# Group 0's second part moved behind group 10, and side work held to the program's order on VectorE, in a hybrid decoder layer

## The chip, the core and the metric

The kernel runs on one core of one Trainium2 chip. A core has five engines that work from queues of their own: TensorE (PE in the profile; its weight loads are PEld), VectorE (DVE), ScalarE (ACT), GpSimd (POOL) and SyncE (SP), which here issues all DMA transfers. The metric is the device time of one execution in microseconds; the time of a kernel is the median of several runs.

## The reference

One decoder layer on x of 1024 tokens by 1024 channels, float32: a first feed-forward (SwiGLU, inner width 2816) with half weight, a mixer, a second feed-forward with half weight, and a final norm. Each of the three sub-layers has a norm whose scale, shift and gate come from the conditioning vector.

```python
h = modulate(rms_norm(x, ffn1_norm[l]), sh1, sc1)
x = x + 0.5 * g1 * swiglu(h, w_gate, w_up, w_down)     # (silu(h @ w_gate) * (h @ w_up)) @ w_down
h = modulate(rms_norm(x, mix_norm[l]), sh2, sc2)
b_gate, c_gate, v, u = split(h @ w_in)
y_conv = b_gate * causal_conv3(c_gate * v)
y_ssm  = glu(gelu(s5_scan(u)))                          # diagonal complex state, 32 groups x 64 states
x = x + g2 * (concat(rms_norm(y_conv), rms_norm(y_ssm)) @ w_out)
h = modulate(rms_norm(x, ffn2_norm[l]), sh3, sc3)
x = x + 0.5 * g3 * swiglu(h, ...)
return rms_norm(x, final_norm)
```

## The kernel before

Data lies with channels on the 128 partitions and tokens along the row, in two halves of 512 tokens (`h` = 0, 1). Every float32 matrix product is three matmuls of a high and a low part (`mm3`): each weight tile and each activation is split by ScalarE (a cast to the high part) and VectorE (the rest). The weights come through `Weights`: raw arrays of 1 MB (`raw`, two buffers), split tiles of two chunks (`w`, a ring of three, with a fourth, `ring1`, in some stages), in the order in which the stages take them.

The inner width is cut into eleven groups of 256. In the first feed-forward groups 0 to 3 are plain products (`gate_up`), groups 4 to 10 use a scheme of seven products in place of eight on the two halves of tokens and of channels (`seven`; its operands are called A11, A12, A22 and S1 to S4, its PSUM banks A to E; GpSimd forms the sums of the weights). What a group gives is stored to DRAM scratch (`kept`) and fetched again (`fetch`) for the second part, the product with the down weights. Groups 1 to 8 go through `down7` in two chunks of four groups (fad0, fad1; again seven products each, for two halves p of the output columns). Groups 0, 9 and 10 go through `last_parts` (fald), three weights to one PSUM bank. Each result is added to x on VectorE with the gate. Fetched tiles lie in two pools of buffers, A (20) and B (12), which also hold the activations of the running stage.

Beside the main chain runs side work, written as Python generators: `side1` prepares the tables of the state space part (`ssm_base`, `ssm_batch`), the sums S1 to S4 of the activations (`combos`, `combos_last`), and the gate of the first feed-forward; `side2` computes scales, shifts and gates of later norms, one reduction over a loaded tile `wm` at a time (24 in the first feed-forward's second part, 24 in the mixer, the latter through two buffers). A `Clock` counts the products `mm3` as ticks; after every `period` ticks it takes one step of the side work, so that its instructions are written into the program between those of the main chain. The period is 4 in groups 1 to 3, 7.75 in groups 4 to 10, 8 in chunk 1 and in the last gates of the mixer, 1000 from the mixer's GLU to the middle of the output product, and 3 from there on.

What the program's order means: a scheduler walks the traced instructions at build time with estimated durations and fixes each engine's queue. An instruction that it finds ready may pass an earlier one of the program that waits. On the chip each queue then runs strictly in that order. The wrapper `InOrder` around each engine can bind every instruction to the one before it (`strict`, used in the prologue). Elsewhere nothing is bound: side work may pass the main chain's instructions on VectorE.

The lines in question: `Clock.step` (80), `InOrder.__getattr__` (105), `stream` (287), `seven` (575), `down7` (655), `down2` (700), the stage from line 1173 to 1237, and the mixer's side work from 1413 to 1486.

Of the kernel before, what the change touches and what calls it, by code (L numbers as in the profile page):

```python
# [21 lines left out]
P = 128  # L22
# [16 lines left out]
LAST = ((0, NGRP - 2, NGRP - 1), (NGRP - 2, NGRP - 1))  # L39
# [19 lines left out]
class Clock:  # L59
# [3 lines left out]
    def __init__(self, period):  # L63
        self.now, self.period, self.n, self.since = 0, period, 0, 0
        self.due, self.side = [], deque()
# [31 lines left out]
class InOrder:  # L97


    strict = False  # L100

    def __init__(self, tc, engine):
        self.tc, self.engine, self.last = tc, engine, None

    def __getattr__(self, name):
        def call(*args, **kw):
            r = getattr(self.engine, name)(*args, **kw)  # L107
# [124 lines left out]
def hymba_layer(ctx: ExitStack, tc, x_d, wm1_d, wmod_d, gu1_d, gs1_d, ds1_d, wl1_d, win_d, wout_d, glu_d, gu2_d, gs2_d, wd2_d, ds2_d, wl2_d, cols_d, cond_d, lam_d, bc_d, out_d):  # L232
# [54 lines left out]
    def stream(gu, gs, wd, ds, wl, m):  # L287
# [4 lines left out]
        for g in range(m, NGRP):  # L292
            j = len(srcs)
            inner = g == 1
# [14 lines left out]
    stream(gu1_d, gs1_d, None, ds1_d, wl1_d, SEVEN_FROM[0])  # L309
# [525 lines left out]
    kept = {g: kept_for(g, g not in LAST[0]) for g in range(NGRP)}  # L835
# [337 lines left out]
    movs["B"] = es1.enter_context(tc.tile_pool(name="movB1", bufs=12))  # L1173
# [7 lines left out]
    a_last = [{} for _ in LAST[0]]  # L1181
# [5 lines left out]

    def fetch_last(left):

        if left in ("A11", "A12", "A22"):  # L1190
            i = ("A11", "A12", "A22").index(left)
            for h in range(2):
                for fi in range(2):
                    a_last[i][fi, h] = fetch(kept[LAST[0][i]], f"A{h + 1}{fi + 1}", "A", f"fa{LAST[0][i]}l")

    for g in range(SEVEN_FROM[0], NGRP):
        if g == NGRP - 1:
# [14 lines left out]
    sums_open.close()  # L1212
    ring1_open = ExitStack()

    def last_parts():
        for dh in range(2):
            wd = ws.take(3)
            for h in range(2):
                outs = [ps(f"fald{4 * dh + i}_{h}") for i in range(4)]
                for q, (w, a) in enumerate(zip(wd, a_last)):  # L1220
                    for fi in range(2):
                        for i, o in enumerate(outs):
                            mm3(o[:], w, 4 * fi + i, a[fi, h], q == fi == 0, q == 2 and fi == 1)
                    if h:
                        ws.free()
                for i, o in enumerate(outs):
                    d = 4 * dh + i
                    V.scalar_tensor_tensor(out=x[d][h], in0=o[:], scalar=gate[:, 0, d : d + 1], in1=x[d][h], op0=ALU.mult, op1=ALU.add)
                    after1(d, h)

    last_parts()
# [3 lines left out]
    ring1 = ring1_open.enter_context(tc.tile_pool(name="ring1b", bufs=1, side="right"))  # L1235
    ws.open(ring1, 1)
    ws.pump()
# [247 lines left out]
    clock.period = 4  # L1485
    mods_open.close()
# [40 lines left out]
    kept = {g: kept_for(g, g not in LAST[1]) for g in range(1, NGRP - 1)}  # L1527
# [70 lines left out]
def _arrays(i):  # L1598
# [5 lines left out]
    for n in (1, 2):  # L1604
# [5 lines left out]
        if n == 2:  # L1610
            a["wd2"] = b[0].transpose(1, 2, 0, 3).reshape(P, 2, 1024)
        b = b[list(LAST[n - 1])].transpose(3, 0, 2, 1, 4).reshape(-1, 2, P, 1024)
# [30 lines left out]
_ORDER = ["x", "wm1", "wmod", "gu1", "gs1", "ds1", "wl1", "win", "wout", "glu", "gu2", "gs2", "wd2", "ds2", "wl2", "cols", "cond", "lam", "bc"]  # L1643
# [17 lines left out]
```

## Time and profile before

| what | value |
| --- | --- |
| median of three runs | 1750.19 us (1748.85 to 1751.76) |
| profiled execution | 1752.1 us |
| its span | 1750.3 us |
| granted TensorE clock, mean | 0.989 |
| TensorE busy | 1677.9 us (96%) |
| VectorE busy | 1300.6 us (74%) |
| ScalarE, GpSimd busy | 566.0 us, 351.1 us |
| DMA moved | 304.54 MB, mean 174 GB/s |

How to read it. The profile is of one execution; times in its rows count from the start of the span. The span in 40 slices gives each engine's share in tenths. The waits name who waited, for whom, how long in total, how often, and the longest. A timeline row has its start, its duration, engine, line, operation, output and inputs, and in brackets the idle time before it with what ended it. All main instructions are issued by the helper on line 107, so tiles tell them apart: fa are tiles of the first feed-forward's groups, fad and fald its second part, u, v, c, b, gl, wo the mixer's products, fb the second feed-forward. The prologue runs to 87 us, groups 1 to 10 to 505, the second part to 734, the mixer to 1076.

### The profile page before, as it was taken

To read this page: it belongs to the slowest core of one execution; us is meant where nothing else is said; L and a number is where in the kernel's file an instruction comes from. 1 tells how busy PE (TensorE), PEld (TensorE's weight loads), DVE (VectorE), ACT (ScalarE), POOL (GpSimd) and SP (SyncE) were. 2 spreads that over 40 slices of the span, in tenths; PEclk is the share of its full clock that TensorE was granted. 3 is DMA by queue.
4 is the path that set the end of the run, shared out by engine and by line. 5 is a ranking of instruction groups with operands and counts; after the bars stand their busy time and mean duration, and the time that the engine had idled before them with its cause. 6 is when DMAs were issued, how large, how long until landed. Compare 5 with 4: busy or idle time off the path is not lost.

```text
span 1750.3 us, 20808 instructions
## 1 busy us (share of the span) xinstructions
PE 1677.9 (96%) x7532; PEld 1379.6 (79%) x7532; DVE 1300.6 (74%) x2286; ACT 566.0 (32%) x934; POOL 351.1 (20%) x241
## 2 busy tenths in 40 slices
PE   4999999999999999999999899989999999999996
PEld 3788887878787888887877778778888888888886
DVE  7999999999855687744656977967777666676656
ACT  4223234444322221332113424423343443322221
POOL 0000132222222221100000022023323322333211
PEclk9999999999999999999999999999999999999998
DMA  8245544444597877134654450113444334669312
GB/s 319 85 145 196 207 167 165 182 169 178 196 391 266 326 256 292 56 84 149 210 157 140 144 191 25 48 46 135 157 162 173 147 133 156 239 242 366 115 49 96
DMA packets 101080, 304.54 MB, mean 174 GB/s; under 512 B 19057, under 2 KB 34673, under 8 KB 89842
## 3 DMA queue, kind: packets, MB, share of 16 engines
q1 hardware_dynamic: 100978, 303.22, 48.4%
q8 instruction: 59, 0.97, 0.2%
q14 instruction: 43, 0.35, 0.1%
HBM read 212.47 MB, written 86.51 MB: 171 GB/s over the span
## 4 chain that ended last, share of the span: by engine, by line
PE 76%; DVE 14%; DMA 5%; issue 2%; POOL 1%; ACT 1%; SPq 1%; DVEq 0%; POOLq 0%; ACTq 0%
PE wo L107 4%; PE fald L107 3%; DVE w L107 3%; PE p L107 2%; PE fb10d L107 2%; PE fbd_0B L107 2%; PE fbd_1B L107 2%; PE u L107 2%; DMA swz<-si 2%; PE b L107 1%; DVE x L107 1%; PE c L107 1%; PE fa3u L107 1%; PE fb0g L107 1%; PE fa2g L107 1%
## 5 line engine op out<-in xcount | busy, mean ns | idle before, releaser
L107 ACT CAST w<-raw 128x512 fp32r<-128x512 f32 (+1 forms) x358 | 236.2, 689 | 484.3 <-issue 75.0
L107 DVE TENSOR_TENSOR w<-raw,w 128x512 fp32r<-128x512 f32 (+1 forms) x358 | 295.9, 845 | 107.3 <-ACT w L107 106.5
L164 POOL TENSOR_TENSOR sums<-raw 128x512 f32<-128x512 f32 x50 | 71.4, 1429 | 451.5 <-DMA raw<-in_gs 263.3
L173 POOL TENSOR_TENSOR raw<-sums,raw 128x512 f32<-128x512 f32 x50 | 77.7, 1554 | 371.1 <-DVE w L107 358.9
L175 POOL TENSOR_TENSOR raw<-raw 128x512 f32<-128x512 f32 x50 | 77.5, 1549 | 89.6 <-DVE w L107 73.0
L107 DVE CUSTOM_DVE_ANT_0 wm<-wm,cact 128x1024 f32<-128x1024 f32 x56 | 76.6, 1375 | 16.9 <-DMA wm<-in_wmod 16.9
L165 POOL TENSOR_TENSOR raw<-raw 128x512 f32<-128x512 f32 x50 | 77.3, 1547 | 3.2
L366 POOL TENSOR_TENSOR n3aq<-n3aq,n3aq 128x512 f32<-128x512 f32 x5 | 8.3, 1666 | 281.4 <-DMA wm<-in_wmod 255.7
L107 PE MATMUL p<-h,w 128*128 128x512 f32 x192 | 50.0, 423 | 8.0 <-DVE h L107 5.1
L107 DVE TENSOR_TENSOR w<-sums,w 128x512 fp32r<-128x512 f32 x50 | 52.5, 1063 | 3.6 <-ACT w L107 3.0
L107 PEld LDWEIGHTS p<-h,w 128*128 128x128 f32 x192 | 39.4, 207 | 18.4 <-DVE h L107 6.4
L107 PE MATMUL v<-h,w 128*128 128x512 f32 x192 | 46.9, 395 | 0.0
L107 PE MATMUL c<-h,w 128*128 128x512 f32 x192 | 46.6, 395 | 0.0
L107 PE MATMUL wo<-oa,w 128*128 128x512 f32 x192 | 45.6, 392 | 0.9 <-DVE w L107 0.7
L107 PE MATMUL b<-h,w 128*128 128x512 f32 x192 | 45.6, 394 | 0.0
L107 PE MATMUL wo<-ob,w 128*128 128x512 f32 x192 | 45.5, 392 | 0.0
L107 PE MATMUL u<-h,w 128*128 128x512 f32 x192 | 44.7, 392 | 0.2 <-DVE h L107 0.2
L107 PEld LDWEIGHTS wo<-oa,w 128*128 128x128 f32 x192 | 35.8, 188 | 9.0 <-DVE w L107 1.1
L107 PEld LDWEIGHTS u<-h,w 128*128 128x128 f32 x192 | 35.7, 188 | 8.2 <-DVE h L107 0.6
L107 PEld LDWEIGHTS wo<-ob,w 128*128 128x128 f32 x192 | 35.8, 188 | 7.7 <-DVE ob L107 0.4
L107 PEld LDWEIGHTS b<-h,w 128*128 128x128 f32 x192 | 35.6, 188 | 7.1
L107 PEld LDWEIGHTS c<-h,w 128*128 128x128 f32 x192 | 35.4, 188 | 7.0
(1565 smaller groups left out, 4056.2 us busy)
## 6 DMA issues: line engine op xcount, KB each, us to landing
raw<-in_gs SPq DMA_DIRECT2D x34, 1024.0 KB, 5.5
wm<-in_wmod SPq DMA_DIRECT2D x56, 512.0 KB, 5.3
raw<-in_ds SPq DMA_DIRECT2D x16, 1024.0 KB, 7.2
raw<-in_gu SPq DMA_DIRECT2D x10, 1024.0 KB, 7.0
mw<-in_wm SPq DMA_DIRECT2D x8, 1024.0 KB, 12.8
x<-in_x SPq DMA_DIRECT2D x16, 512.0 KB, 8.0
raw<-in_win SPq DMA_DIRECT2D x8, 1024.0 KB, 5.4
raw<-in_wl SPq DMA_DIRECT2D x5, 1024.0 KB, 6.7
```

Of the source, the lines that this page charges most:

```text
L107: r = getattr(self.engine, name)(*args, **kw)
L164: self.G.tensor_tensor(out=f, in0=r[2], in1=r[1], op=ALU.subtract)
L165: self.G.tensor_tensor(out=r[1], in0=r[1], in1=r[0], op=ALU.subtract)
L173: self.G.tensor_tensor(out=r, in0=s["t3"], in1=r, op=ALU.add)
L175: self.G.tensor_tensor(out=r, in0=self.chunk(j, 3), in1=r, op=ALU.subtract)
L366: nc.gpsimd.tensor_tensor(out=a, in0=a, in1=sq[:, :n], op=ALU.add)
```

## The change

Three things change in the first feed-forward and the mixer; the second feed-forward is as before.

First, group 0 leaves the last parts. Its second part is a stage of its own directly behind group 10 (`down2`, both halves, weights `wd1` of 1 MB). Its four stored tiles are fetched where chunk 0's A11 was fetched, and that fetch now follows the new stage. The last parts hold groups 9 and 10 alone and go through `down`: half 0 with all eight output tiles, then half 1, with four weight tiles taken at once; the fourth ring tile is opened ahead of it. The period in chunk 1 and the last parts is 7 in place of 8.

Second, all eight transfers of x are issued before group 10, in place of four there and four in chunk 0.

Third, `Clock.step` marks VectorE as pinned while a side step is traced, from group 1 to the end of the mixer's side work. A pinned instruction is bound, without a semaphore, to the VectorE instruction traced just before it. Main instructions are not bound.

```diff
-LAST = ((0, NGRP - 2, NGRP - 1), (NGRP - 2, NGRP - 1))
+LAST = (NGRP - 2, NGRP - 1)
...
     def step(self):
         if self.side:
+            if self.pin is not None:
+                self.pin.pinned = True
             try:
                 next(self.side[0])
             except StopIteration:
                 self.side.popleft()
+            if self.pin is not None:
+                self.pin.pinned = False
...
-            if self.last is not None and InOrder.strict:
+            if self.last is not None and (InOrder.strict or self.pinned):
...
+        if m > 1:
+            plain([wd])
...
+    clock.pin = V
     for g in range(1, SEVEN_FROM[0]):
...
+    def fetch_all(tiles, g):
+        for h in range(2):
+            for fi in range(2):
+                tiles[fi, h] = fetch(kept[g], f"A{h + 1}{fi + 1}", "A", f"fa{g}l")
+
+    def fetch_now(left):
+        if left == "A11":
+            fetch_all(a_first, 0)
+        else:
+            fetch_chunk(0, left)
...
-            load_x(range(2), (0, 2))
+            load_x(range(2))
...
-        seven(f"fa{g}", lambda: None, kept=kept[g], then=(lambda left: fetch_chunk(0, left)) if g == NGRP - 1 else None)
-    down7("fad0", lefts[0], 0, lambda left: fetch_chunk(1, left), lambda left: load_x(range(2), (1, 3)) if left == "A12" else None)
-    clock.period = 8
+        seven(f"fa{g}", lambda: None, kept=kept[g], then=fetch_now if g == NGRP - 1 else None)
+    down2(a_first, 0, "fa0", (0, 1))
+    fetch_chunk(0, "A11")
+    down7("fad0", lefts[0], 0, lambda left: fetch_chunk(1, left))
+    clock.period = 7
...
     sums_open.close()
+    movB1_open.close()
     ring1_open = ExitStack()
-    last_parts()
+    ring1 = ring1_open.enter_context(tc.tile_pool(name="ring1b", bufs=1, side="right"))
+    ws.open(ring1, 1)
+    ws.pump()
+    w = ws.take(4)
+    for h in range(2):
+        down(h, [w[0], w[2], w[1], w[3]], a_last, 0, "fal", after1)
+    ws.free(4)
...
     clock.period = 4
+    clock.pin = None
     mods_open.close()
```

The helpers it calls stood there before. `down2` takes two weight tiles and, for each output tile, makes two products of one PSUM bank and adds the bank to x; `down` fills four banks at a time over both groups and adds them to x, each followed by `after1`, which adds the squares for the next norm.

More of the change, by code (lines that the diff above doesn't have):

```diff
@@ L64, in __init__ @@
         self.now, self.period, self.n, self.since = 0, period, 0, 0
-        self.due, self.side = [], deque()
+        self.due, self.side, self.pin = [], deque(), None
     def after(self, ticks, fn):
@@ L102, in __init__ @@
     def __init__(self, tc, engine):
-        self.tc, self.engine, self.last = tc, engine, None
+        self.tc, self.engine, self.last, self.pinned = tc, engine, None, False
     def __getattr__(self, name):
@@ L833, in kept_for @@
         return {left: scratch.tile([P, 2, HALF], F32, name=f"kept{g}{left}") for left in names}
-    kept = {g: kept_for(g, g not in LAST[0]) for g in range(NGRP)}
+    kept = {g: kept_for(g, 0 < g < NGRP - 2) for g in range(NGRP)}
     afs = {}
@@ L1180, in hymba_layer @@
     lefts = [{left: [] for left, _ in SEVEN} for _ in range(CHUNKS)]
-    a_last = [{} for _ in LAST[0]]
+    a_first, a_last = {}, [{} for _ in LAST]
     HOMES = dict(A11="A", S2="B", A12="A", S3="B", S1="B", A22="A", S4="A")
@@ L1186, in fetch_chunk @@
             lefts[c][left].append(fetch(kept[g], left, HOMES[left], f"{name}{g}l"))
-    def fetch_last(left):
[L1190 to L1194, printed above, removed]
+    def fetch_all(tiles, g):
[7 more added lines that the diff above has]
+            fetch_chunk(0, left)
+    def fetch_last(left):
+        if left in ("A11", "A12"):
+            i = ("A11", "A12").index(left)
+            fetch_all(a_last[i], LAST[i])
     for g in range(SEVEN_FROM[0], NGRP):
@@ L1212, in hymba_layer @@
     sums_open.close()
+    movB1_open.close()
     ring1_open = ExitStack()
[L1215 to L1229, printed above, removed]
-    last_parts()
+    ring1 = ring1_open.enter_context(tc.tile_pool(name="ring1b", bufs=1, side="right"))
[5 more added lines that the diff above has]
+    ws.free(4)
     while clock.side:
@@ L1526, in hymba_layer @@
     a_prev = group0()
-    kept = {g: kept_for(g, g not in LAST[1]) for g in range(1, NGRP - 1)}
+    kept = {g: kept_for(g, g not in LAST) for g in range(1, NGRP - 1)}
     HOMES = dict(A11="B", S2="A", A12="B", S3="A", S1="B", A22="A", S4="A")
@@ L1640, in _arrays @@
     return {k: np.ascontiguousarray(v) for k, v in a.items()}
-_ORDER = ["x", "wm1", "wmod", "gu1", "gs1", "ds1", "wl1", "win", "wout", "glu", "gu2", "gs2", "wd2", "ds2", "wl2", "cols", "cond", "lam", "bc"]
+_ORDER = ["x", "wm1", "wmod", "gu1", "gs1", "wd1", "ds1", "wl1", "win", "wout", "glu", "gu2", "gs2", "wd2", "ds2", "wl2", "cols", "cond", "lam", "bc"]
 def kernel(**inputs):
```

17 lines of the change are left out of this document (7 added, 10 removed).

## The prediction

> **What bounds the kernel now.** I read the page's share of busy time and its 40 slices first.
>
> ```profile
> span 1750.3 us, 20808 instructions
> ...
> PE 1677.9 (96%) x7532; PEld 1379.6 (79%) x7532; DVE 1300.6 (74%) x2286; ACT 566.0 (32%) x934; POOL 351.1 (20%) x241
> ...
> PE   4999999999999999999999899989999999999996
> ...
> DVE  7999999999855687744656977967777666676656
> ```
>
> TensorE is busy 1677.9 of 1750.3 us. The change alters no matmul's shape or number, so only the gaps are at stake. Next, the waits of TensorE; columns: total us, times, longest.
>
> ```profile
> PE fb0d L107 <- DVE x L107: 5.1, 4, 2.0
> ...
> PE nBabc L107 <- DVE nBarb L107: 3.9, 1, 3.9
> ...
> PE fa7gC L107 <- DVE fa7gt L107: 2.6, 1, 2.6
> ...
> PE fa5uC L107 <- DVE fa5ut L107: 2.1, 1, 2.1
> ...
> PE fa9gC L107 <- DVE fa9gt L107: 1.2, 1, 1.2
> ```
>
> VectorE stands behind nearly all of them. Then stages by windows: length, busy us of PE, PEld, DVE, ACT, POOL, granted clock, DMA share, GB/s.
>
> ```profile
> 71.00:92.00 21.00, 21.00 (x94) 17.41 (x93) 19.09 (x94) 7.74 (x13) 0.00 (x0) 1.00 0.18 35
> 92.00:218.00 126.00, 126.00 (x562) 104.14 (x561) 121.83 (x359) 38.51 (x60) 8.45 (x5) 1.00 0.53 186
> 218.00:467.27 249.27, 243.39 (x1099) 198.34 (x1099) 231.60 (x360) 98.68 (x177) 74.72 (x48) 0.99 0.48 172
> ...
> 505.35:543.43 38.08, 38.08 (x169) 31.21 (x167) 23.54 (x34) 8.19 (x15) 2.13 (x3) 1.00 0.93 346
> 543.43:562.62 19.19, 15.33 (x49) 11.13 (x49) 10.79 (x11) 5.06 (x10) 11.35 (x8) 0.82 0.51 189
> 950.00:990.00 40.00, 32.41 (x140) 26.26 (x140) 33.74 (x74) 16.80 (x26) 0.00 (x0) 0.91 0.41 132
> 1016.00:1048.00 32.00, 31.12 (x136) 25.19 (x135) 20.48 (x28) 4.43 (x6) 10.21 (x5) 1.00 0.62 215
> 1048.00:1078.00 30.00, 30.00 (x142) 25.08 (x141) 21.92 (x43) 11.86 (x17) 6.63 (x4) 1.00 0.00 1
> ```
>
> In groups 1 to 9 of the first feed-forward (92 to 467) VectorE has 4.2 + 17.7 = 21.9 us idle in 375. From 505 the DMA engines are 93% busy, and the next stretch is the costliest in what the change touches.
>
> **Part 1: group 0's second part moves.** Thirty-two products of three matmuls leave the last parts and stand directly behind group 10.
>
> ```profile
> 98.08 10.88 PE fa1u L107 x48
> ...
> L107 PE MATMUL fald<-fa0lA,w 128*128 128x512 f32 x96 | 22.8, 392 | 0.6 <-DVE w L107 0.5
> ...
> L107 DVE SCALAR_TENSOR_TENSOR x<-fald,gate,x x16: 746/751/751, 683.2 to 744.8; 128x512 f32<-128x512 f32 x16
> ```
>
> One matmul takes 10.88/48 = 0.227 us, so 96 take 21.8 us in either place: zero. But they put 21.8 us between group 10 and the first sevenfold product (down7, chunk 0), which is where 543 to 562 goes wrong: there 48 matmuls (10.9 us) take 19.2 us, 8.3 us lost, partly waiting and partly at clock 0.82. The cause is late weights for its second half:
>
> ```profile
> 532.35 0.54 SPq L107 DMA_DIRECT2D x<-in_x  x1
> 532.98 1.28 SPq L107 DMA_DIRECT2D raw<-in_ds  x2
> ...
> 543.07 0.62 ACT L107 CAST w<-raw 128x512 fp32r<-128x512 f32 x1 [14.26 <-DMA raw<-in_ds]
> ...
> raw<-in_ds SPq DMA_DIRECT2D x2, 1024.0 KB, 10.9
> ...
> raw<-in_ds SPq DMA_DIRECT2D x2, 1024.0 KB, 8.2
> ...
> 625.00:640.00 15.00, 13.86 (x62) 11.16 (x61) 11.94 (x16) 4.81 (x9) 10.40 (x7) 1.00 0.44 169
> ```
>
> The two raw arrays are issued at 533, behind fetches, and land 10.9 us later. At the same seam of chunk 1 (8.2 us to land) only 1.1 us is lost (15.00 - 13.86). With 21.8 us more for the fetches the first seam should look like the second: 8.3 - 1.1 = 7.2 gained at best, nothing if the queue is still full. The queue also gets more: four fetches of group 0's activations (2 MB) and one raw array (1 MB) come ahead instead of later, all x loads stand before group 10's fetches (in the trace the last goes out at 532), and A11's four fetches of chunk 0 are now issued after the new stage. At 346 GB/s, 3 MB are 9 us of the 21.8. I take -6 us (ends -7.2 and 0).
>
> What it adds: sixteen more updates of x, 16 x 0.75 = 12 us of VectorE, under 21.8 us of matmuls, while group 10's tail is still to be written. In the second feed-forward the same stage (fb0d) waits 5.1 us for x. In 505 to 543 VectorE is 62% busy. Ends 0 and +5.1; I take +1.5. A11's late fetch: it has the whole new stage to land, but its buffers come free only as group 10's four stored tiles leave; a fetch that misses its place costs up to the 5.0 us that VectorE sat for one here: ends 0 and +5, +0.5 taken.
>
> ```profile
>   DMA fa2lA<-kept2A: 5.0, 1
> ```
>
> ```profile
> 1013.90 2.43 DVE L107 TENSOR_TENSOR w<-raw,w 128x1024 fp32r<-128x1024 f32 x2
> ```
>
> The last parts become 64 products, half 0 entirely before half 1, with all four weight tiles held to the end. The norm of half 0 gets 32 products of cover instead of 24; the price is that two of the four weights of the mixer's first product can be split only after the last matmul, while the other two have 16 products (10.9 us) ready. Ends -0.5 (the wait of fald above) and +3 (two splits like this row's, 2.4 us, and a cast ahead of them); +0.5 taken. ring1's earlier opening and the period of 7 go with it: 176 ticks at 7 give 25 steps for 24 reductions.
>
> **Part 2: pinning in groups 1 to 9.** A pinned side operation may not start before the vector operation ahead of it in the program.
>
> ```profile
> 71.29 0.11 DVE L107 TENSOR_SCALAR w<-lam 128x32 f32<-128x32 f32 x1
> ...
> 87.04 3.34 PE L107 MATMUL fa1g<-h,w 128*128 128x512 f32 x14
> ```
>
> The first side arithmetic runs at 71.3, but its step belongs eight ticks (5.4 us) into group 1, at about 92.5. So up to the 19.1 us of VectorE in 71 to 92 move behind 92, into 21.9 us of idle of which 4.2 lie in the next 126 us. The total fits, the place hardly. Twelve points in groups 4 to 9 show pressure: the second use of bank C waits for the vector add that reads the first. Three of them stalled, 2.6 + 2.1 + 1.2 = 5.9 us. Ends: -5.9 (main operations come first and all three go) and +14.9 (19.1 - 4.2, what the early stretch can't take). I take +4, nearer to a doubling of the stalls, since VectorE is 93 to 97% busy there. If side work ends later than now, x loads wait too; their cover is the new stage's own start at 505.
>
> **Part 3: pinning in the mixer.** Twenty-four reductions over modulation weights (wm) are the side work.
>
> ```profile
> 975.15 0.16 DVE L107 TENSOR_SCALAR nBanv<-nBast 128x4 f32<-128x4 f32 x1 [0.23 <-PE nBast L107]
> ...
> 975.89 1.22 DVE L107 CUSTOM_DVE_ANT_0 wm<-wm,cact 128x1024 f32<-128x1024 f32 x1
> ...
> 981.81 1.22 DVE L107 CUSTOM_DVE_ANT_0 wm<-wm,cact 128x1024 f32<-128x1024 f32 x1
> ...
> 983.15 0.43 DVE L107 COPY nBarb<-nBany 128x512 f32<-128x512 f32 x1
> ...
> 1018.49 1.21 DVE L107 CUSTOM_DVE_ANT_0 wm<-wm,cact 128x1024 f32<-128x1024 f32 x1
> ...
> 1048.16 1.23 DVE L107 CUSTOM_DVE_ANT_0 wm<-wm,cact 128x1024 f32<-128x1024 f32 x1 [1.08 <-DMA wm<-in_wmod]
> ...
> 1050.72 2.79 DVE L107 SCALAR_TENSOR_TENSOR x<-wo,gate,x 128x512 f32<-128x512 f32 x4 [0.92 <-PE wo L107]
> ...
> 1064.81 1.41 DVE L107 SCALAR_TENSOR_TENSOR h3t<-x,scl,n3abc 128x512 f32<-128x512 f32 x2
> ...
> 1076.18 5.60 PE L107 MATMUL fb0g<-h,w 128*128 128x512 f32 x24
> ...
> L107 DVE CUSTOM_DVE_ANT_0 wm<-wm,cact x24: 1214/1221/2310, 955.5 to 1048.2; 128x1024 f32<-128x1024 f32 x24
> ```
>
> Four reductions belong to the gates' steps; then the period of 1000 stops the steps, and twenty belong behind the weight split of the row quoted above, which ends at 1013.90 + 2.43 = 1016.3. Today the fifth runs at 975.9: three reductions (3 x 1.22 = 3.7 us) stand inside nBa's chain, for which TensorE waited 3.9 us. Pinned, they leave: ends -3.9 and 0, and the half clock in that window (0.91) can add to it; I take -4.
>
> The price: twenty reductions start at 1016 at the earliest. From 1018.49 to 1048.16 ten ran, 29.67/9 = 3.3 us apart, set by two buffers and their loads. Twenty need 19 x 3.3 = 63 us, so they end near 1079 instead of 1048. Queued behind them on VectorE are the x updates at 1050.7 and half 0's norm, whose first h3t is at 1064.8 for a product at 1076.2. If all stand ahead, that chain starts 1079 - 1051 = 28 us late against about 10 us of slack: +18; if none does, 0. I take +8, since only the last eight (the gates) come into question and main operations may overtake those that are not ready.
>
> In 1016 to 1048 GpSimd is busy 10.2 us, in 950 to 990 not at all, and a reduction there takes up to 2.31 us against 1.22. The Trainium skill, page "SBUF — State Buffer", section "Who interferes with whom", says that a VectorE instruction with two SBUF inputs and a GpSimd instruction that reads SBUF exclude each other for the whole instruction. By that rule the reductions are moved from a free into a contended stretch, and 1.1 us on up to half of the moved twenty would put the forecast about 11 us higher at worst; the trace agrees with the rule, and the cadence of 3.3 us already holds such cases.
>
> **Sum.** -6 + 1.5 + 0.5 + 0.5 + 4 - 4 + 8 = +4.5 us. The profiled execution took 1752.1 us (span 1750.3), 0.1% above the median of 1750.19, which stands for the runs; forecast 1754.7, said as 1755.
>
> **The rivals.**
> Faster: the reductions stay hidden because the norm's operations overtake the gates', and pinning lets main operations first. Then -6 + 2.5 - 2 (one stall of three gone) - 4 = -9.5: 1741. For it: DMA waits before wm cost VectorE idle time now without TensorE waiting more than 0.9 us in 1016 to 1048 (32.00 - 31.12). Against it: 63 us of cadence in 60 us of stage. It decides at whether half 0's norm starts within 10 us of where it does.
> VectorE becomes the bound in groups 1 to 9: +14.9 instead of +4, so 1766. For it: 4.2 us idle in 126. Against it: TensorE does not wait there at all today.
> The seam doesn't heal, as the queue is as full as before: part 1 is +2.5 instead of -3.5, so 1761 with the rest as forecast.
> No net change: the seam pays for the late reductions, 1748 to 1753.
>
> **How the numbers follow.** A measurement of this kernel tells about 0.2% (3.5 us) from nothing. Forecast 0.29, healed-not 0.07, VectorE bound 0.13: slower 0.49. Faster rival 0.34. No net change 0.17. The low end goes a little below the faster rival's 1741, the high end to VectorE bound: 1739 to 1767; slower cases alone, 1754 to 1767.
>
> **What would show it.** Seam: the sevenfold product's second half (12 matmuls per bank) without waits for w and at clock 1.0. New stage: waits of its matmuls for x under 2 us. Pinning: first side arithmetic after 90 instead of 71; sum of the C waits above 5.9. Mixer: no wm inside nBa's chain, its wait under 1 us; wm ending past 1065 and fb0g's first product waiting for h. The prediction is wrong if fb0g starts straight after wo, or if groups 4 to 9 lose their C waits.

## The result and the profile after

The changed kernel takes 1802.82 us (median of 4 runs, 1798.85 to 1804.81) against 1749.52 us for the kernel before (median of 4 runs, 1745.65 to 1751.76): a ratio of 1.0304, 95% interval 1.0277 to 1.0331. Slower was the likelier side of the prediction, but 1755 us and its range up to 1767 us are missed by far.

The page of the changed kernel, total busy time and the slices:

```profile
span 1802.5 us, 20840 instructions
...
PE 1688.4 (94%) x7532; PEld 1385.5 (77%) x7532; DVE 1316.7 (73%) x2302; ACT 567.1 (31%) x934; POOL 356.8 (20%) x241
...
PE   4999979999994999999999999989999999999997
...
DVE  7799799899963669783566777886667766576656
```

A slice is 45 us. TensorE has two new dips, in the sixth slice (225 to 270 us) and the thirteenth (541 to 586 us). VectorE stood at nine tenths from the second slice to the tenth before; now the second and the fifth (45 to 90 and 180 to 225 us) have fallen to seven. The waits of TensorE in the changed kernel (total us, times, longest):

```profile
PE fad_0A L112 <- DMA fa1lA<-kept1A: 23.4, 1, 23.4
...
PE kp L112 <- DVE bl L112: 4.8, 3, 3.1
PE n3ast L112 <- DVE n3aq L112: 4.4, 1, 4.4
...
PE fa5gC L112 <- DVE fa5gt L112: 3.5, 1, 3.5
...
PE fa4gB L112 <- DVE w L112: 2.8, 1, 2.8
...
PE fa6gC L112 <- DVE fa6gt L112: 2.4, 1, 2.4
PE n3bbc L112 <- DVE n3brb L112: 2.2, 1, 2.2
PE fa4uB L112 <- DVE fa4gu L112: 2.1, 1, 2.1
```

One wait of 23.4 us stands alone: the first product of chunk 0 (fad_0A) waits for the first fetched A11 tile. The rest are many small waits for VectorE in groups 4 to 9, and two in n3, the norm in front of the second feed-forward, which is formed during the mixer. By windows of the changed kernel (length, busy us of PE, PEld, DVE, ACT, POOL, granted clock, DMA share, GB/s):

```profile
71.00:218.00 147.00, 147.00 (x655) 121.44 (x654) 118.18 (x416) 44.52 (x69) 4.18 (x3) 1.00 0.36 125
218.00:275.00 57.00, 45.42 (x176) 34.65 (x175) 54.31 (x86) 19.11 (x35) 16.03 (x9) 0.88 0.57 203
275.00:495.70 220.70, 206.00 (x916) 165.87 (x915) 202.99 (x314) 82.49 (x146) 67.69 (x42) 0.98 0.46 162
533.80:555.60 21.80, 21.80 (x97) 17.83 (x95) 14.02 (x20) 1.25 (x2) 4.42 (x4) 1.00 1.01 409
555.60:579.10 23.50, 0.14 (x2) 0.06 (x1) 5.64 (x7) 3.32 (x6) 4.29 (x3) 0.61 0.74 272
579.10:734.00 154.90, 154.90 (x672) 127.97 (x673) 110.17 (x151) 35.90 (x61) 37.96 (x24) 0.98 0.66 252
```

The six rows tell the story in order: groups 1 to 3 run at full speed while VectorE does less work than before (118.18 us); group 4 (218 to 275) loses 11.6 us of TensorE time and works at clock 0.88; groups 5 to 9; the moved stage without a gap; the stall; chunks 0 and 1 without a gap. Stage by stage, from the first and last matmul of each in both traces:

| stage | before, us | after, us | difference |
|---|---|---|---|
| start of group 1 | 87.0 | 85.0 | -2.0 |
| groups 1 to 3 | 132.2 | 132.2 | 0 |
| group 4 | 39.7 | 58.4 | +18.7 |
| groups 5 to 9 | 208.3 | 220.2 | +11.9 |
| group 10 | 38.1 | 38.1 | 0 |
| stall in front of chunk 0 | 0 | 23.5 | +23.5 |
| chunks 0 and 1 | 162.3 | 154.9 | -7.4 |
| group 0's part and the last parts | 68.1 | 21.8 + 45.4 | -0.9 |
| mixer | 340.3 | 342.7 | +2.4 |
| first stage of the second feed-forward | 45.4 | 50.6 | +5.2 |
| all behind it | 628.7 | 629.8 | +1.1 |

The differences sum to 52.5 us, the spans differ by 52.2. So two things are to be explained, 31 us in groups 4 to 9 and 23.5 us in front of chunk 0. Of group 4's 18.7 us, 11.6 are waiting, and the other 7.2 are matmuls that take longer: from its first matmul to group 5's, TensorE is busy for 46.78 us with the 181 matmuls that took 39.60 before, at clock 0.88 in place of 1.00. The mixer's 2.4 us say little by themselves, since that stage takes 336.6 to 342.2 us in the eleven runs of this document that pin nothing there; the 5.2 us behind it are clear of this, since that stage takes 45.4 us in all of those.

### The profile page after: what moved, and what is told of

It is laid out like the page before. It is cut to its first block, busy times and chain, and to the rows that moved or that the text cites. A ratio compares the mean times of both kernels' runs of the same rounds, so it can differ in the third digit from the quotient of the medians.

```text
span 1802.5 us, 20840 instructions
## 1 busy us (share of the span) xinstructions
PE 1688.4 (94%) x7532; PEld 1385.5 (77%) x7532; DVE 1316.7 (73%) x2302; ACT 567.1 (31%) x934; POOL 356.8 (20%) x241
## 4 chain that ended last, share of the span: by engine, by line
PE 70%; DVE 21%; DMA 5%; issue 2%; ACT 1%; SPq 1%; POOL 0%; DVEq 0%; ACTq 0%; POOLq 0%
DVE w L112 3%; PE p L112 2%; PE fb10d L112 2%; PE wo L112 2%; PE fbd_1B L112 2%; PE fbd_0B L112 2%; PE fad_1B L112 2%; PE fad_0B L112 2%; PE u L112 2%; DVE x L112 2%; PE fald L112 2%; PE b L112 1%; DVE wm L112 1%; PE v L112 1%; DMA swz<-si 1%
## 5 line engine op out<-in xcount | busy, mean ns | idle before, releaser
L169 POOL TENSOR_TENSOR sums<-raw 128x512 f32<-128x512 f32 x50 | 75.9, 1518 | 511.6 <-DMA raw<-in_gs 273.1
L112 DVE CUSTOM_DVE_ANT_0 wm<-wm,cact 128x1024 f32<-128x1024 f32 x56 | 74.4, 1332 | 14.0 <-DMA wm<-in_wmod 13.8
L112 DVE TENSOR_TENSOR w<-sums,w 128x512 fp32r<-128x512 f32 x50 | 55.0, 1113 | 27.6 <-ACT w L112 27.0
```

Of the source, the lines that this page charges most:

```text
L169: self.G.tensor_tensor(out=f, in0=r[2], in1=r[1], op=ALU.subtract)
```

## The experiments

### Which part costs what

Three kernels take the change apart, and a fourth tries a first cause for the stall. Theory 1: the pin costs the 31 us, the late fetch the stall, and the moved stage itself gains. Theory 2: the moved stage costs the 31 us too. Theory 3: the pin makes the stall.

The move alone, `e1_move_alone`:

```diff
     clock.period = 4
-    clock.pin = V
     for g in range(1, SEVEN_FROM[0]):
```

> The changed kernel without any pinning: group 0's second part behind group 10 stays, the side work is free again. Theory 1 (pinning costs some 30 us in groups 4 to 9, the late A11 fetch some 20 us behind the new stage, and the moved stage itself gains its 7 us): groups 1 to 10 take the time of before and the stage fa4 about 40 us instead of 58; the stall of fad_0A on the A11 tiles stays, 18 to 23 us, because the cast of the third kept10A tile still stands behind casts of weights in ScalarE's queue; in all 1762 us (1757 to 1768). Theory 2 (the moved stage and its buffers cost the 31 us in groups 4 to 9 too, by memory or by the ring of weights): fa4 stays at 55 us or more and the time near 1795. Theory 3 (the pinned order also causes the A11 stall): the stall falls below 8 us and the time to 1747 or less.

Measured: 1762.67 us against 1748.89, ratio 1.0081 (1.0066 to 1.0096). Group 4 takes 39.7 us, and the stall is there with 18.4 us. This is theory 1 in place and size; theories 2 and 3 fall, though the other 5 us of the stall come with the pin.

The pin alone, put into the kernel before together with the change's lines in `Clock.step` and `InOrder`, `e2_pin_alone` (the line that ends the pin behind the mixer isn't shown):

```diff
     clock.period = 4
+    clock.pin = V
```

> The kernel before with the pinning alone, in the first feed-forward and the mixer; group 0's second part stays with the last parts. Theory 1: fa4 takes 55 to 60 us, groups 4 to 9 some 30 us more than before, no stall on A11 above 2 us, and the mixer about as in the changed kernel: 1784 us (1776 to 1790). Theory 2: below 1765, since the 31 us belong to the moved stage. Theory 3: the late fetch shows here too, over 10 us in front of fad_0A, and the time passes 1795.

Measured: 1797.77 us, ratio 1.0276 (1.0259 to 1.0293), 14 us more than theory 1 said. Group 4 takes 58.7 us and groups 1 to 10 31.7 us more than before, as expected. The surplus lies at the old seam (chunks 0 and 1 take 169.8 instead of 162.3 us, with fad_0A waiting 6.2 us for weights) and from the mixer's first product to the end of the second feed-forward's first stage (396.9 instead of 385.7).

The move, and the pin from chunk 1 on only, `e3_move_late_pin`:

```diff
     clock.period = 7
+    clock.pin = V
     clock.side.append(side2(mod_mov, (SC2, SH2, G2)))
```

> The move with the pinning only from fad1 on, so in the mixer and not in groups 1 to 10. Against the move alone this prices the mixer's pin. Theory 1: the wait of nBabc falls from 3.9 to about 0.7 us, the third modulation's reductions come later and cost n3ast and the first stage of the second feed-forward 4 to 8 us: 0 to 6 us slower than the move alone, 1765 us. The rival, that those 5 us in the second feed-forward's first stage come from the move: the move alone shows them too, and this run is 3 to 4 us faster than it.

Measured: 1766.80 us, ratio 1.0104 (1.0089 to 1.0119): 4.1 us slower than the move alone. Chunk 1 and the last parts gain 3.5 us, the wait of nBabc falls from 3.9 to 0.7, and from the mixer's first product to the end of the second feed-forward's first stage 7.6 us are lost (384.9 to 392.5). The first stage of the second feed-forward is 45.4 us in the move alone and 50.6 here, so its 5 us belong to the pin.

So the move costs 13.8 us and the late pin 4.1. What is left, 36.0 us from here to the changed kernel (1802.82 - 1766.80), is found in the traces: 30.6 us in groups 4 to 9 and 5.0 in the stall.

### The stall in front of chunk 0

SyncE's queue in the changed kernel, around the stall (start, duration, what is issued):

```profile
547.83 0.32 SPq L112 DMA_DIRECT2D fa4lA<-kept4A  x1
561.54 0.32 SPq L112 DMA_DIRECT2D kept10A<-fa10A  x1
...
568.37 0.32 SPq L112 DMA_DIRECT2D fa1lA<-kept1A  x1
...
572.76 0.32 SPq L112 DMA_DIRECT2D fa4lA<-kept4A  x1
```

From 548 to 561 nothing is issued: the store of group 10's third tile waits. The four fetches of A11, needed first, go out last. My first theory was that pause. ScalarE's order has the cast of that tile behind casts of weights that wait for a slot of the ring, so `e4_act_order` holds ScalarE to the program's order:

```diff
             load_x(range(2))
+            A.pinned = True
...
     fetch_chunk(0, "A11")
+    A.pinned = False
```

> The changed kernel with ScalarE's queue held to the program's order from group 10 to the fetch of A11: only there, and its one effect on that queue is that the casts of group 10's last two kept tiles come ahead of three casts of weights that wait for the ring. Theory 1 (two queues in order, one behind the other, make the A11 fetch late): the store of the third kept10A tile is issued near 540 instead of 561.5, A11 is fetched as soon as the new stage's tiles come free (549 to 556), the stall of fad_0A falls from 23.4 to 3 to 10 us, and the time to 1785 us (1780 to 1790). The rival (the buffers of group 0's tiles or the time to land set the fetch): the stall stays above 18 us and the time within 5 us of the changed kernel's. What could be lost: weights cast later, so waits of fa0d and fad_0 for w.

Measured: 1799.55 us, ratio 1.0294 (1.0276 to 1.0313), stall 18.7 us. This theory's stall of 3 to 10 us did not come. The cast came early, and the store still went out at 560.84: now its last rounding on VectorE stood behind all sixteen x updates of the moved stage. So `e5_both_orders` holds both engines:

```diff
-            A.pinned = True
+            A.pinned = V.pinned = True
```

> The changed kernel with both ScalarE's and VectorE's queue held to the program's order from group 10 to the fetch of A11, since with ScalarE's alone the last rounding of the third kept10A tile stood behind the new stage's sixteen x updates on VectorE and its store was still issued at 560.8. Theory 1 (that blocked store makes A11 late): SP's pause of 10 to 13 us in front of the store is gone, and the stall of fad_0A falls below 10 us; 1785 us. The rival (volume: 28 tiles of 512 KB stand ahead of A11 in the queue and the DMA engines move them at 1.2 us each whatever the order, DMA share 1.03 and 413 GB/s): the pause is gone, but the last A11 tile is still issued after 563 and lands after 573, and the stall stays at 14 us or more; 1795 us.

Measured: 1797.48 us, ratio 1.0295 (1.0279 to 1.0310). The pause is gone, and little is won. The same queue, in this run:

```profile
551.43 0.32 SPq L112 DMA_DIRECT2D kept10A<-fa10A  x1
...
564.77 0.32 SPq L112 DMA_DIRECT2D fa1lA<-kept1A  x1
...
568.51 0.32 SPq L112 DMA_DIRECT2D fa4lA<-kept4A  x1
```

And the window around it, in this run:

```profile
548.00:575.00 27.00, 15.76 (x61) 12.65 (x62) 13.66 (x20) 2.44 (x5) 8.27 (x6) 0.75 1.03 420
```

Without any pause the fetches go out every 1.25 us ((568.51 - 564.77) / 3), since the DMA engines are full: share 1.03, 420 GB/s. Group 10 ended at 537.4 here, 3.6 us later than in the changed kernel; counted from there the first product starts after 37.5 instead of 45.3 us. The moved stage itself takes 21.8 us, so 15.7 us of lateness stay without the pause. (Most of it is hidden in this run, since the pinned order made the moved stage wait 12.8 us for x.) My first theory falls in the main: by this run the pause costs some 8 us, the volume ahead of A11 some 16.

If it is the volume, another order of the same fetches must heal it. `e6_move_fetch_order` is the move alone with A11 fetched fourth of the chunk's seven operands, behind S2, S3 and S1, and S4, needed last, in A11's old place:

```diff
-            fetch_chunk(0, left)
+            fetch_chunk(0, dict(S1="S2", S2="S3", S3="S1", A12="A11", A22="A12", S4="A22")[left])
...
-    fetch_chunk(0, "A11")
+    fetch_chunk(0, "S4")
```

> The move without any pinning, and the fetches of the first product chunk put in another order: S2, S3, S1 in the places of S1, S2, S3, A11 in A12's place, A12 in A22's, A22 in S4's, and S4, which is needed last, behind the new stage in A11's place. The same tiles, bytes and buffers; no queue pinned. By the volume rival A11 is issued near 508 to 512 instead of 532 to 538, lands by 523, before the new stage ends at 525, and the stall of fad_0A (18.4 us in the move alone) is gone but for 0 to 3 us; then A12 behind the store of the third kept10A tile may cost the third product 0 to 5 us: 1746 us (1743 to 1752). If A11's lateness comes from its buffers, the stall stays where it was and the time at 1760 or more.

Measured: 1742.02 us, ratio 0.9972 (0.9963 to 0.9981). SyncE's queue and then TensorE in this run:

```profile
507.77 0.32 SPq L112 DMA_DIRECT2D fa1lA<-kept1A  x1
...
511.59 0.32 SPq L112 DMA_DIRECT2D fa4lA<-kept4A  x1
...
503.85 21.92 PE L112 MATMUL fa0d<-fa0lA,w 128*128 128x512 f32 x96
525.61 0.84 PE L112 MATMUL fad_0A<-fa1lA,w 128*128 128x512 f32 x3
```

A11 is under way before the moved stage is far into its work, and the first product follows the moved stage without a wait. The store of group 10's third tile holds the queue for 13.7 us in this run too (nothing leaves between 512.82 and 526.47), and it costs nothing, since A11 is already ahead of it. So this run shows that the order decides; how the stall splits between volume and pause rests on `e5` alone. The move in this order is faster than the kernel before. The same two lines in the changed kernel, all pinning kept (`e12_after_fetch_order`):

> The changed kernel as it is, all its pinning kept, with the new order of fetches alone. If volume and order of the fetches make the whole stall of 23.4 us, it goes: 1780 us (1776 to 1786). If the pinned order has a part in it by itself, for which the 5 us between 23.4 and 18.4 speak, some 5 us stay: 1785.

Measured: 1779.74 us, ratio 1.0176 (1.0162 to 1.0190): 23.1 us won, so the whole stall, the pin's 5 us in it included.

### The pin in groups 1 to 9

First by place: pinned only while groups 1 to 3 are issued, `e7_pin_1_3`, and only from group 4 to the end of the side work, `e8_pin_4_9`, both on the kernel before:

```diff
     clock.period = 4
+    clock.pin = V          # e7
...
     clock.period = 7.75
+    clock.pin = None       # e7;  V in e8, None ahead of chunk 0
```

> The kernel before, with the side work pinned only while groups 1 to 3 are issued, free from group 4 on. Theory (the loss is deferral: VectorE does 15 instead of 94 instructions at 71 to 92 us and 108 instead of 122 us of work up to the end of group 3, and this work comes back in groups 4 to 9 where VectorE is full): fa4 still takes 50 us or more, groups 4 to 9 cost 22 to 31 us; 1775 us (1770 to 1782). Rival (the order inside groups 4 to 9 costs it): below 1755.

Measured: 1770.89 us, ratio 1.0141 (1.0124 to 1.0158). Group 4 takes 57.6 us.

> The kernel before, with the side work pinned only from group 4 on to the end of the first feed-forward. Deferral theory: 0 to 8 us slower, 1749 to 1757, fa4 below 45 us. The rival: fa4 at 50 us or more and 1772 or more. If each half alone costs over 15 us, both hold.

Measured: 1768.56 us, ratio 1.0133 (1.0116 to 1.0150). Group 4 takes its 39.7 us, but groups 5 to 9 lose 10.6 us, and chunks 0 and 1 lose 9.0 at the old seam, where fad_0A waits 7.6 us for weights. So both halves cost; the seam part does not arise in the changed kernel, whose seam has healed.

Is the price of the first half work put off? VectorE's work between 71 and 218 us points to it; first the row of the kernel before:

```profile
71.00:218.00 147.00, 147.00 (x655) 121.55 (x654) 140.92 (x452) 46.25 (x72) 8.45 (x5) 1.00 0.48 164
```

The changed kernel did 118.18 us in the same stretch (above), 22.7 us less, though TensorE was equally busy. VectorE idles in two stretches there, rows of the changed kernel:

```profile
81.91 0.69 DVE L112 TENSOR_TENSOR fa<-fa,p 128x512 f32<-128x512 f32 x1 [12.10 <-PE p L112]
...
91.44 0.17 DVE L112 TENSOR_SCALAR w<-lam 128x32 f32<-128x32 f32 x1
...
194.11 0.69 DVE L112 TENSOR_TENSOR fa<-fa,fa3u 128x512 f32<-128x512 f32 x1 [4.82 <-PE fa3u L112]
...
200.81 0.69 DVE L112 TENSOR_TENSOR fa2S<-fa,fa2S 128x512 fp32r<-128x512 f32 x1 [4.61 <-ACT fa2S L112]
```

The first lies in front of group 1: VectorE waits 12.1 us for TensorE's product p, and the first side arithmetic (on lam), which ran at 71.3 before, starts at 91.44. The second lies between 186 and 201 us. If pinned work merely stood too late in the program, more of it earlier should help: `e9_pin_1_3_denser` gives the pinned side work a step every 2 ticks.

```diff
-    clock.period = 4
+    clock.period = 2
     clock.pin = V
```

> The kernel before with the pinning in groups 1 to 3 as in the run before of that kind, but a step of side work every 2 ticks instead of every 4 while it is pinned, so the same work stands earlier in the program's order. Deferral theory: VectorE's idle time in groups 1 to 3 fills again, the backlog does not reach group 4, fa4 falls from 57.6 to 40 to 45 us, and the time to 1752 us (1748 to 1760). The rival (a pinned queue costs as such, since side work in it waits for what stands ahead of it and makes main work late): no better than 1768, or the 1 to 3 groups themselves get longer by 5 us and more.

Measured: 1801.00 us, ratio 1.0291 (1.0275 to 1.0306), so my expectation fell. VectorE still idled at 71 to 83; then the pinned steps stood ahead of group 1's and 2's own work, and one wait of TensorE (fa2u for the activation of fa) took 24.1 us. So denser is not earlier in the first stretch, and behind it steps that came too early cost 28.3 us in groups 1 to 3, while group 4 still took 53.5.

So I cut the first half: only the base of the state-space tables pinned (`e13_pin_base`), and only what follows it in groups 1 to 3 (`e14_pin_rest_1_3`).

```diff
             yield from ssm_base(sb1)
+        clock.pin = None     # e13
+        V.pinned = False     # e13
+        clock.pin = V        # e14, not pinned before
```

(Not shown: both set the pin to None where group 4 starts, and `e13` sets it to V where group 1 starts.)

> The kernel before with the pin only on the first piece of side work, the base of the state-space tables (some 270 small instructions), free from the combinations on. By deferral only the first hole should stand (VectorE idle 13.6 us in front of the first product of group 0's second half, 71 to 83 us); up to group 4 the kernel before leaves VectorE about 6 us idle, so some 8 of the 13.6 us reach group 4. If the hole itself is the price: 5 to 12 us slower, 1755 to 1761, fa4 at 44 to 50 us. If the scheduler fills what it frees: within 3 us of before.

Measured: 1773.78 us, ratio 1.0152 (1.0135 to 1.0169), more than the 1755 to 1761 expected. Both idle stretches of VectorE are there, with nothing pinned at the second.

> The kernel before with the pin in groups 1 to 3 but not on that first piece. Only the second hole should stand (186 to 206 us, 12.2 us of waits for fa3u and for casts of fa2S, with the first batch pinned behind them). If the hole itself is the price: fa4 at 46 to 55 us and 8 to 15 us slower, 1757 to 1764. If it needs both holes: within 5 us of before. By additivity this run and the other together lose the 22 us of the pin in groups 1 to 3.

Measured: 1756.98 us, ratio 1.0054 (1.0039 to 1.0068). The long second stretch is not there, only a wait of 4.1 us, and 8.6 us are lost. The larger part is the base, then, and something of the base reaches to 186 us. It is found in SyncE's queue. The instructions on the tile `zero`, before:

```profile
L107 SPq DMA_DIRECT2D mk_d<-zero x56: 549/592/1689, 71.4 to 144.2; - x56
L107 DVE MEMSET zero<- x1: 152/152/152, 71.2 to 71.2; 16x112 f32 x1
```

and after the change:

```profile
L112 SPq DMA_DIRECT2D mk_d<-zero x56: 557/592/966, 149.3 to 185.2; - x56
L112 DVE MEMSET zero<- x1: 152/152/152, 149.1 to 149.1; 16x112 f32 x1
```

This MEMSET, the base's last instruction, depends on nothing. Free, it runs at 71.2 and its 56 stores go out in pieces; pinned, it runs behind all of the base, and the stores fall into SyncE's queue as one block. SyncE's queue of the changed kernel (start, duration of the group):

```profile
149.30 36.53 SPq L112 DMA_DIRECT2D mk_d<-zero  x56
185.94 0.52 SPq L112 DMA_DIRECT2D kept2A<-fa2A  x1
...
188.96 0.44 SPq L112 DMA_DIRECT2D prm<-in_bc  x1
```

For 36.5 us nothing else leaves: neither group 2's tiles nor weights nor the parameters of the first batch, which the kernel before fetched at 152.07. What is blocked is the queue, not the DMA engines: from 149.30 to 185.83 their share is 0.19, against 0.59 in the same stretch of the kernel before. Three runs test it. In the changed kernel the MEMSET alone is freed (`e15_after_zero_free`); in the kernel before it alone is pinned (`e16_zero_alone`); and `e18_base_zero_free` pins the base without it, which leaves only VectorE's first idle stretch. The lines that free it:

```diff
+        last, was, V.pinned = V.last, V.pinned, False   # e15, e18
         V.memset(zero[:], 0.0)
+        V.last, V.pinned = last, was
```

> The changed kernel with one instruction freed from its pinning: the MEMSET of the tile zero (0.15 us), from which 56 stores into mk_d go out. In the kernel before it runs at 71.2 us, since it waits for nothing, and its stores go out in pieces up to 144 us; pinned, it runs at 149.1 us behind all of the base, and the 56 stores block SP's queue in one piece for 36.5 us, with kept2A's and kept2S's stores, a fetch of weights, two of modulation and the first batch's parameters behind them. Theory (that block is the main price of the pin in groups 1 to 9): the second idle stretch of VectorE (186 to 206 us) goes, fa4 falls from 58.4 to 39 to 45 us, and the time from 1802.8 to 1780 to 1790; what stays is the A11 stall, the mixer's 4 us and 8 to 17 us of groups 4 to 9. Rival (VectorE's first idle stretch, 71 to 83 us, is the price): fa4 stays above 50 us, 1795 or more.

Measured: 1797.13 us, ratio 1.0273 (1.0258 to 1.0289). Group 4 falls from 58.4 to 43.1 us, but group 3 rises by 7.6 and groups 5 to 9 by 2.8, and only 5.7 us are won. Group 4 does what the theory said, the time what the rival said: with all the other pins in place the block is not the main price.

> The kernel before with nothing pinned but that one MEMSET. The rest of the base may still run early on VectorE, so the first idle stretch (13.6 us) stays filled. Theory of the blocked queue: 15 to 25 us slower than before, 1764 to 1774, fa4 at 50 us or more, the second idle stretch there without the first. Rival: within 5 us of before, 1744 to 1754.

Measured: 1763.89 us, ratio 1.0083 (1.0068 to 1.0098): one instruction of 0.15 us, made to wait until 130.3 us, costs 14.5 us. The first stretch stays filled; the second is there, with 10.8 us of waiting in one piece in front of 188.8. This run's row:

```profile
71.00:218.00 147.00, 147.00 (x656) 121.40 (x655) 124.71 (x418) 46.30 (x72) 7.34 (x4) 1.00 0.41 143
```

> The kernel before with the base pinned as in the run that cost 25 us, but the MEMSET of zero free. SP's 56 stores go out in pieces from 69 us on; VectorE's first idle stretch (13 us at 71 to 83) stays, alone. If it has a price of its own, as the 24.8 us that stay up to the end of group 10 with the MEMSET freed in the changed kernel suggest: 6 to 14 us slower than before, 1755 to 1763, most of it in fa4 and fa5. If VectorE's later slack takes it up: within 4 us of before.

Measured: 1763.60 us, ratio 1.0090 (1.0064 to 1.0117). This run's row:

```profile
71.00:218.00 147.00, 146.40 (x652) 120.89 (x652) 129.18 (x437) 42.76 (x66) 7.17 (x5) 1.00 0.46 155
```

So both stretches have their price, and each brings the backlog by itself. What VectorE did less in 71 to 218 us than before, from this row of each run, beside what groups 1 to 10 took longer (first matmul of group 1 to last of group 10; 418.2 us before):

| run | pinned | VectorE less, us | groups 1 to 10 longer, us |
|---|---|---|---|
| `e18` | base without the MEMSET | 11.7 | 13.9 |
| `e16` | the MEMSET alone | 16.2 | 15.3 |
| `e13` | base | 27.3 | 24.7 |
| `e7` | all in groups 1 to 3 | 24.8 | 22.3 |
| `e14` | the rest of groups 1 to 3 | 8.0 | 7.2 |
| `e8` | all from group 4 on | 0.1 | 10.6 |
| changed kernel | all | 22.7 | 30.6 |
| `e15` | all but the MEMSET | 21.8 | 25.6 |
| `e9` | all in groups 1 to 3, steps twice as dense | 27.6 | 55.3 |

In the first five rows, where nothing from group 4 on is pinned, TensorE pays 0.9 to 1.2 us for each us that VectorE did not work before group 4. `e9` loses 28.3 of its 55.3 us in groups 1 to 3 themselves; the other 27.0 fit, too. From group 4 on the pin itself costs 10.6 us alone (`e8`) and 8.3 on top of the first half's (30.6 - 22.3). `e15` doesn't fit so well: VectorE did only 1.0 us more there than in the changed kernel, and groups 1 to 10 gained 5.0 us.

`e17_after_zero_fetch` joins the freed MEMSET and the new order of fetches in the changed kernel:

> The changed kernel with that MEMSET freed and the new order of fetches, all other pinning kept. If both causes add up: 1779.7 less what the MEMSET is worth in the run beside it, so 1757 to 1767, and the seam gains its 7 us. What then stands above the 1742.0 us of the move without pinning in groups 1 to 10 is the pin's own price, the mixer's 4 us included.

Measured: 1773.74 us, ratio 1.0146 (1.0119 to 1.0173), 6.0 us better than the new order alone, the same as in `e15`. The two causes add, but the expected 1757 to 1767 was too good: the MEMSET is worth 14.5 us alone and 6 us where the rest is pinned too. How the rest divides between the first stretch and the later pins within the full pin stays open.

### Can the mixer's pin be kept?

Both on the move with the new order of fetches, unpinned in groups 1 to 10. `e10_best_pin_sooner` pins from chunk 1 to the mixer's end and gives the third modulation's steps a shorter period:

```diff
+    clock.pin = V                 # from chunk 1
...
-    clock.period = 8
+    clock.period = 4              # third modulation's steps
...
-    clock.period = 3
+    clock.period = 2
```

> The move without pinning in groups 1 to 10, with the new order of fetches (1742.0 us), and with the pin from fad1 to the end of the mixer, where the third modulation's steps come every 4 ticks instead of 8 ahead of the gated part and every 2 instead of 3 behind it. If the mixer pin's price (7.6 us between u and fb0, of it n3ast 4.3 us and n3bbc 2.3) is late reductions, both waits shrink, the gain at nBabc (3.9 to 0.7 us) and the 3.5 us at fad1 and the last parts stay: 1737 us (1734 to 1742). If not, 1746.

Measured: 1745.81 us, ratio 0.9981 (0.9972 to 0.9990). The wait of n3bbc is gone and the second feed-forward's first stage is back at 45.4 us, but more reductions now stand near nBa's chain (nBabc waits 5.4 us, n3ast still 3.5): from the mixer's first product to the end of that stage it takes 394.1 us, against 384.3 in `e6`. `e11_best_pin_ff1_end` pins chunk 1 and the last parts only:

```diff
     while clock.side:
         clock.step()
+    clock.pin = None
     es1.close()
```

> The same with the pin only from fad1 to the last parts, none in the mixer. The stages from u on take the time of the move alone; fad1 and the last parts gain 0 to 3.5 us over the 1742.0 us: 1739 us (1738 to 1743).

Measured: 1736.13 us, ratio 0.9930 (0.9918 to 0.9943). This kernel is ahead of `e6` and `e10`: it has the move, the new order of fetches, and the pin only where it gained.

## Why the prediction was wrong

**The seam was right.** It forecast -6 (ends -7.2 and 0) for the weights that came late to chunk 0's second half; chunks 0 and 1 gained 7.4 us and have no wait left (154.90 us busy of 154.90). The stall in front gave their weights time, but it isn't the cause: without it the two chunks take 154.3 us in `e6` and 155.4 in `e12`, against 162.3 before. The new stage's waits for x (+1.5) did not come: 21.80 us busy of 21.80. The last parts (+0.5) gained 0.9 with the stage that left them, and this is the pin's doing: unpinned they take 47.0 (`e1`) and 48.0 us (`e6`) in place of 45.4, a loss of 0.7 and 1.7.

**"A11's late fetch: it has the whole new stage to land"** is the first step that failed: +0.5 with ends 0 and +5, measured 23.4 us, 18.4 of it without any pin. The sum had counted what the queue gets more (3 MB) and not what stands ahead of A11. From group 0's first tile on that is 28 tiles and four stores of 512 KB and one raw array of 1 MB, 17 MB in binary units, or an estimated 44 us at the 401 to 409 GB/s of that stretch. Measured from the first fetch to A11's, it is 40.6 us without the pause (`e5`, 524.20 to 564.77) and 47.8 with it (520.54 to 568.37), and a tile of A11 then takes some 10.6 us to land; the stage meant to cover this takes 21.8. The upper end of 5 us was taken from a wait of VectorE on one fetch, a row that knows nothing of the queue's volume.

**"Pinning in groups 1 to 9 ... I take +4"** is the second: about 31 us, twice the upper end of 14.9. The mechanism behind that end was right: the first side arithmetic starts at 91.44, as forecast, and VectorE's idle stretch in front of group 1, alone, cost 15.7 us (`e18`, 1763.60 against 1747.94); the 21.9 us of idle time later gave nothing back. That 15.7 lies so near to 14.9 is partly luck, since VectorE did 11.7 us less there, not 14.9. What the step lacked is that a pinned step also issues DMAs. The one MEMSET carries 56 stores, and held back it blocked SyncE's queue for 36.5 us, worth 14.5 us alone (`e16`) and 5.7 beside the other pins (`e15`). Nor had it a price for pins from group 4 on (10.6 us alone, `e8`). The lower end, which had main operations go first, was wrong in direction: the waits at bank C rose from 5.9 to 13.0 us. And bank C was all it looked at; the waits came at the weights, at the batches' matmuls (kp) and at bank B as well, and the granted clock fell to 0.88 in group 4.

**The mixer** was right in direction. -4 for nBa's chain: its wait fell from 3.9 to 0.7 us. +8 for late reductions: from the end of the gate's products (gl) to the end of the second feed-forward's first stage 12.8 us were lost (133.0 us in the move alone, 145.8 with the late pin), within its end of +18. But the place differed: fb0g did start straight behind the last wo, which the text had named as a sign of being wrong; the wait came earlier, at n3ast (4.4 us), and later, at n3bbc (2.2). The gain of 3.5 us at chunk 1 and the last parts was not foreseen. In the changed kernel the reductions run like this:

```profile
L112 DVE CUSTOM_DVE_ANT_0 wm<-wm,cact x24: 1211/1222/2311, 997.1 to 1113.6; 128x1024 f32<-128x1024 f32 x24
```

Their median is 1222 ns against 1221 before. Four of the 24 run long (1.93 to 2.31 us), each while GpSimd works on n3, against three before; the long ones exceed 1.22 us by 3.6 us in all, against 3.3. So single reductions agree with the rule on contention from the Trainium skill, "SBUF — State Buffer", section "Who interferes with whom", and the 11 us by which it might have raised the forecast did not come.

**The rivals.** "VectorE becomes the bound" named the right place at half the size. "The seam doesn't heal" and "faster" were both wrong for the change as made; the faster one's 1741 is what the move reaches once A11 is fetched in time (1742.0) and no pin stands in groups 1 to 10, but by the seam, not by the rival's reasons, so the match is chance. "No net change" was wrong by 50 us.

## What to carry to other kernels

Where a change puts a stage between two others, list for the first tile it then waits for all that stands ahead of it in the DMA queue, in bytes, and divide by the rate that the trace shows at full share; the order of fetches has to follow the order of use. Where a change fixes the order of an engine's instructions, look for those that depend on nothing: the free order had them early, and what they release (stores above all) moves with them into other queues. Idle time of a nearly full engine is only worth something ahead of the work that needs it: here each us that VectorE did not work before group 4 came back as about one us of TensorE time, although VectorE had slack later (202.99 us busy of 220.70 in groups 5 to 9).

## What the runs showed of the hardware

Fifty-six small stores occupy SyncE's queue for 36.53 us, 0.65 us each, although the largest writes 64 x 112 numbers (29 KB) and the DMA engines' share is 0.19 meanwhile; a fetch of 512 KB takes 1.25 us of the same queue. Those 1.25 us are the DMA engines' own pace (share 1.0, 401 to 420 GB/s): after a pause of 13.7 us the next ten left within 6.8 us (561.5 to 568.4) in place of 12.5, so the queue made up some 5.7 of the 13.7. The first three matmuls behind the 23.4 us stall took 1.62 us against 0.84 us for the same three without a stall, at a granted clock of 0.61 in the stretch that holds the stall. In the changed kernel the row is:

```profile
579.07 1.62 PE L112 MATMUL fad_0A<-fa1lA,w 128*128 128x512 f32 x3 [23.36 <-DMA fa1lA<-kept1A]
```
